# A fused attention and FNet layer on one core: fewer idle products ahead of the first latents, a z tile ahead of block one's columns, and pairs of halves that join the tile rotation one piece later

## The chip, the core and the metric

The kernel runs on one core of one Trainium2 chip. The metric is the device time of one execution in microseconds (us); less is better. PE is the matrix engine, DVE the vector engine, ACT the scalar engine, POOL GpSimd and SP the engine that issues most of the DMAs.

## The reference, cut to what matters

One layer, 512 latent tokens and 256 context tokens of 2048 channels, all in float32:

```
ada    = silu(c) @ w_ada + b_ada                    # 2048 -> 3*2048: shift, scale, gate
h      = rmsnorm(x, norm_g) * (1 + scale) + shift   # the latents, 512 x 2048
p      = h @ w_in                                   # q, k, v, z_a, u_b, z_b, g_a, g_b
q, k   = rope(rmsnorm(heads of p)); k, v also of the context
y_a    = (attention(q, k, v) * silu(z_a)) @ w_proj_a
y_b    = (fft2(u_b).real * silu(z_b)) @ w_proj_b
y      = (sigmoid(g_a) * y_a + sigmoid(g_b) * y_b) @ w_out
out    = rmsnorm(x + gate * y, final_g)
```

## The kernel before, in words

**Splitting.** PE gets float32 precision from three products of halves: every operand is split into a high half, which ACT rounds off (L176), and a low half, which DVE takes as the difference (L177). `mm3` (L327 to L329) is the three products. So each piece of weights (128 x 1024) goes through a DMA by SP or POOL, then ACT, then DVE, before PE can use it.

**The start stage**, to about 166 us. xT arrives and ACT and DVE square its rows, two at a time; DVE adds the two squares (L534), and PE adds up over the partitions with a column of ones (`token_norms`, four products of 128 columns for each of eight pairs, L536). Between them stand idle products whose results nobody reads (`warm`, L516, into the PSUM buffer `wacc`). Then come a square root on ACT (L540), a reciprocal on DVE (L541), the first half of the adaptive row for block 0 of the channels (`matvec(0, 0)`, L554), the spreading of the reciprocal root over the partitions (`spread`, L547), and `matvec(0, 1)`. With them `columns(0)` makes two columns, gain and shift (PE transposes in `turned` L575, DVE sums them up in `factors` L586 to L589), and `row_hi`, `scaled` and `row_lo` (L605, L608, L612) make the latents of block 0, high and low half. PE's products for u (four tiles) and z (four tiles, t = 4 to 7) of this block follow (`start_work`, L660 to L663 and L327 to L329). The z tiles go through the two PSUM buffers of `bank3`; `keep` (L635) moves each out, in block 0 by a copy on ACT (L641), later by an addition on DVE (L643). The same is done for blocks 1, 2, 3 and so on up to 15. `some(n)` issues the next n pieces of this work, `modulate(k, split_next)` the two matvecs of block k, a split of a loaded weight piece and the copy of the row (`ado`, L570). Here the order on PE, ACT and DVE is the order of the code, written out by hand (`tc.manual_schedule`).

**The eight groups** follow, g = 0 to 7: seven products with four pieces of weights each (28 pieces a group). PE works 2.74 us on a piece. The tile framework's scheduler sets the order here. A piece's halves are taken from a list that is rotated by one at each split (`hl_tiles`, L239): three pairs of whole tiles, to which at the step Q5 of group 0 two "int tiles" are added (`hl_pools += range(MORE_HL)` in the loop over the groups, MORE_HL = 2). An int tile is a pair of halves in two places, so a piece that gets one is split in two steps of 512 columns on each engine, and its rows are named `s` where those of the others are `whi` and `wlo`. From that point `get` splits up to four pieces ahead (`look`). At the step Q3 of group 4 the int tiles are taken out again, and at the start of group 6 they come back. Some pieces of weights are differences: DVE subtracts one loaded piece from another (L265) before the split, and gate rows are scaled on DVE (L1285) before their split.

Of the kernel before, what the change touches and what calls it, by code (L numbers as in the profile page):

```python
# [22 lines left out]
KK = D // P  # L23
# [96 lines left out]
def block_kernel(ctx, tc, xT, ctx_rows, ctx_toks, x, c_row, w_ss, w_gate, vecs, qkg, rope, dft_c, dft_s,  # L120
                 w_start, w_g, w_pab, w_o, final_g, out):
    nc = tc.nc
# [54 lines left out]
        return first, nc.vector.tensor_tensor(lo, src, hi.bitcast(F32), op=ALU.subtract)  # L177


    todo, ahead = [], []  # L180
    chain, left = [], [0] * 4
    raw_pools, hl_pools = [(wp, RAW, "raw", RAW)], [wp] * HL

# [53 lines left out]
        return [Halves([pairs[2 * n + k][i][:, :, 256:] for k in range(2)]) for i in range(2)]  # L237

    def hl_tiles():  # L239
        hl_pools.append(hl_pools.pop(0))  # L240
        pool = hl_pools[-1]
        if isinstance(pool, tuple):
            return [slot_tile(p, (1024,), F32R) for p in pool]
        if isinstance(pool, int):
            return int_tiles(pool)
        return [pool.tile([P, 1024], F32R, tag=t, bufs=hl_pools.count(pool), name=uid("w" + t)) for t in ("hi", "lo")]
# [266 lines left out]
    def warm(n, src):  # L513

        for _ in range(n):
            nc.tensor.matmul(wacc[:, :256], ones, src, start=True, stop=True)  # L516

    def token_norms():

        t = hm_tile([P, 2, T], F32, name=uid("nm"))  # L520
        pick, r = t[:, 0, :].rearrange("p (t c) -> p t c", t=4), t[:, 1, :P]
        nc.gpsimd.memset(pick, 0.0)
        for t in range(4):
            nc.gpsimd.memset(pick[32 * t : 32 * t + 1, t, :], 1.0)
        acc = bank2()
        for q in range(0, KK, 2):
            two = hm_tile([P, 2, T], F32, name=uid("sq"))
            a, b = two[:, 0, :], two[:, 1, :]
            nc.scalar.activation(a, xt[:, q, :], ACT.Square)
            if q in (6, 10):  # L530
                nc.vector.tensor_tensor(b, xt[:, q + 1, :], xt[:, q + 1, :], op=ALU.mult)
            else:
                nc.scalar.activation(b, xt[:, q + 1, :], ACT.Square)
            nc.vector.tensor_tensor(a, a, b, op=ALU.add)  # L534
            for t in range(4):
                nc.tensor.matmul(acc[32 * t : 32 * t + 32, :P], ones[:, :32], a[:, t * P : t * P + P],  # L536
                                 start=q == 0, stop=q == KK - 2)
            warm(2 if q < KK - 2 else 1, two[:, 0, :256])

        nc.scalar.activation(r, acc[:, :P], ACT.Sqrt, bias=eps_t[:, 0:1], scale=1.0 / D)  # L540
        nc.vector.reciprocal(r, r)  # L541
        return pick, r
# [60 lines left out]
    def row_hi(kb):  # L603
        rows_of(kb)
        nc.scalar.activation(hhi[kb], y_of[kb], ACT.Identity, bias=shift[:, kb, 0:1], scale=gain[:, kb, 0:1])  # L605

    def scaled(kb):
        nc.vector.tensor_scalar(xt[:, kb, :], y_of.pop(kb), gain[:, kb, 0:1], None, op0=ALU.mult)  # L608
# [26 lines left out]
    def keep(t, acc, kb, nk):  # L635
        if held and held[0] is None:
            held[0] = t, acc, kb, nk
            return
        dst = pt(t)
        if kb == 0 or t < 4:  # L640
            nc.scalar.copy(dst, acc)  # L641
        else:
            finals.append(nc.vector.tensor_tensor(dst, acc, dst, op=ALU.add))  # L643
# [41 lines left out]
    def some(n):  # L685
        for _ in range(n):
            next(work)
# [21 lines left out]

    E = mybir.EngineType  # L710
    with tc.manual_schedule(engines={E.PE}):
        norms = token_norms()
        two[0] = bank2()
        matvec(0, 0)
        rx0.append(spread(*norms))
        matvec(0, 1)
        with tc.manual_schedule(engines={E.Activation, E.DVE}):
            nc.scalar.copy(rx, rx0[0])
            by_root(0)
            split_next()  # L720
            taken(0)
            wada[2] = wada_load(2)
            load_start()
            columns(0)
            row_hi(0)
            scaled(0)
            row_lo(0)
            split_next()
            by_root(1)
            some(4)  # L730
            modulate(1, split_next)
            wada[3] = wada_load(3)
            load_start()
            some(2)
            columns(1)
            row_hi(1)
            scaled(1)
            row_lo(1)
            some(2)
            for kb in range(1, 4):  # L740
                k = kb + 1
                some(2 + (kb == 1))
                by_root(k)
                modulate(k, split_next)
                if kb < 3:
                    wada[k + 2] = wada_load(k + 2)
                    load_start()
                hold()
                some(2 - (kb == 1))
                columns(k)  # L750
                row_hi(k)
                release()
                scaled(k)
                if kb < 3:
                    some(2)
                row_lo(k)
                if kb == 3:
                    some(2)
                    by_root(5)
                    modulate(5)  # L760
                    for k in (6, 7):
                        wada[k] = wada_load(k)
                        load_start()
                    hold()
                    some(2)
                    columns(5)
                    row_hi(5)
                    release()
                    scaled(5)
                    row_lo(5)  # L770
                else:
                    some(2)
            for kb in range(4, KK - 4, 2):
                some(3)
                split_next()
                some(5)
                split_next()
                k = kb + 2
                for i in range(2):
                    modulate(k + i)  # L780
                    if k + 2 + i < KK:
                        wada[k + 2 + i] = wada_load(k + 2 + i)
                        for _ in range(2 if k + 2 + i == KK - 3 else 1):
                            load_start()
                some(1)
                for i in range(2):
                    turned(k + i)
                factors(k)
                make_h(k, lambda: some(1))
                factors(k + 1)  # L790
                make_h(k + 1, lambda: some(1))
                if k >= 8:
                    form_row(k - 8)
                    form_row(k - 7)
                some(1)
                if kb == KK - 6:
                    split_table(0)
                    split_from(get(("dftc", 0)), fch[:, 0, :], fch[:, 1, :])
                    load_start()
        some(2)  # L800
        k = KK - 2
        for i in range(2):
            modulate(k + i)
        some(1)
        for i in range(2):
            turned(k + i)
        for i in range(2):
            factors(k + i)
            ins = make_h(k + i)
            with behind(ins):  # L810
                split_next()
                form_row(k + i - 8)
            if not i:
                load_start()
        some(4)
        some(1)
        some(8)
# [499 lines left out]
    for g, kind in enumerate(KINDS):  # L1317
# [13 lines left out]
        for name in ONE_GROUP:  # L1331
# [5 lines left out]
            if (g, name) == (0, "P7"):  # L1337
                raw_pools.remove((rp, 1, "raw0", 1))
            if (g, name) == (0, "Q5"):
                hl_pools += range(MORE_HL)  # L1340
                look[0] = 4
            elif (g, name) == (0, "P2"):

                with tc.issue_after(last_split[-1][1].ins):
                    rotations(HD ** -0.5)
            elif (g, name) == (KV, "P1"):
                load_rotations(qkg[:, 2:4, :], nc.scalar)
            elif (g, name) == (KV, "Q5"):
                with tc.issue_after(last_split[-1][1].ins):
                    rotations(1.0)  # L1350
            elif (g, name) == (KV - 1, "Q3"):
                raw_pools.remove((rp, 1, "raw1", 1))
                hl_pools[:] = [p for p in hl_pools if not isinstance(p, int)]
            elif (g, name) == (KV + 1, "Q6"):
                raw_pools += [(rp, 1, "raw1", 1), (gvp, 2, "raw", 2)]
            elif (g, name) == (LAST, "P7"):
                raw_pools.remove((gvp, 2, "raw", 2))
            elif (g, name) == (LAST, "Q3"):

                free += [(fms[i], f"s{i}") for i in (4, 5, 6, 7, 12, 13, 14, 15, 8, 9, 10, 11, 2, 3, 0, 1)]  # L1360
                for h in range(2):
                    load_head(h)
            elif (g, name) == (LAST, "Q4"):
                hl_pools[:] = [p for p in hl_pools if not isinstance(p, int)]
                get_keys(0)
                jobs.append(lambda: turn_queries(0, pair("y")[:, 0, :]))
# [613 lines left out]
```

## Time and profile before

| | us |
|---|---|
| time before, three runs | 1307.32, 1310.15, 1310.84 (median 1310.15) |
| the profiled execution's own time | 1307.52 |
| its span | 1305.7 |
| PE busy in it | 1278.5 (98%) |
| DVE, ACT, POOL busy | 995.2, 683.6, 167.5 |
| mean granted clock of PE | 0.997 |
| first products with latents: block 0, block 1 | 25.95, 34.30 |

A row of a timeline reads: start, duration, engine, line, operation, output <- input with shapes, count, and in brackets how long the engine stood idle ahead of it and what ended that. A line of the waits reads: engine, what waited <- what for, us in total, times, longest. A line of the table of windows reads: from:to and length, then busy us (and count) of PE, its weight loads, DVE, ACT and POOL, the granted clock, the busy share of the DMA engines (a little over 1 where packets overlap) and GB/s. A line that a helper holds (L177 above all) stands for many places.

### The profile page before, as it was taken

To read this page: it belongs to the slowest core of one execution; us is meant where nothing else is said; L and a number is where in the kernel's file an instruction comes from. 1 tells how busy PE (TensorE), PEld (TensorE's weight loads), DVE (VectorE), ACT (ScalarE), POOL (GpSimd) and SP (SyncE) were. 2 spreads that over 40 slices of the span, in tenths; PEclk is the share of its full clock that TensorE was granted. 3 is DMA by queue.
4 is the path that set the end of the run, shared out by engine and by line. 5 is a ranking of instruction groups with operands and counts; after the bars stand their busy time and mean duration, and the time that the engine had idled before them with its cause. 6 is when DMAs were issued, how large, how long until landed. Compare 5 with 4: busy or idle time off the path is not lost.

```text
span 1305.7 us, 17712 instructions
## 1 busy us (share of the span) xinstructions
PE 1278.5 (98%) x6600; PEld 1051.8 (81%) x6600; DVE 995.2 (76%) x1301; ACT 683.6 (52%) x1078; POOL 167.5 (13%) x220
## 2 busy tenths in 40 slices
PE   7999999999999999999999999999999999999997
PEld 4676888888888788888888888888888888888885
DVE  4756899879687787658687756788798867887676
ACT  5322655555556455444355544666666646464544
POOL 0000011110202111011021010011110212221210
PEclk9999999999999999999999999999999999999998
DMA  9989487888889888977869897477862899998985
GB/s 377 367 353 358 164 244 190 228 238 281 203 276 263 232 299 271 313 200 186 270 202 275 282 227 264 155 229 244 241 230 81 236 248 249 244 212 229 222 204 171
DMA packets 104199, 318.56 MB, mean 244 GB/s; under 512 B 9872, under 2 KB 33040, under 8 KB 100144
## 3 DMA queue, kind: packets, MB, share of 16 engines
q1 hardware_dynamic: 55056, 197.86, 42.1%
q0 software_dynamic: 26736, 97.14, 34.9%
q10 hardware_dynamic: 22320, 22.42, 5.0%
q8 instruction: 52, 0.85, 0.2%
q14 instruction: 35, 0.29, 0.1%
HBM read 283.30 MB, written 34.09 MB: 243 GB/s over the span
## 4 chain that ended last, share of the span: by engine, by line
PE 84%; DMA 5%; DVE 5%; issue 4%; ACT 2%; POOL 0%; ACTq 0%; DVEq 0%; SPq 0%; POOLq 0%
PE banks L327 10%; PE banks L329 9%; PE banks L328 9%; PE x L328 7%; PE x L329 7%; PE x L327 7%; PE y L329 6%; PE y L327 6%; PE y L328 6%; PE pd L554 2%; PE banks L1468 2%; DMA wr<-in_w_g 2%; PE pb L327 1%; PE pb L329 1%; PE pb L328 1%
## 5 line engine op out<-in xcount | busy, mean ns | idle before, releaser
L176 ACT ACTIVATE whi<-R 128x1024 fp32r<-128x1024 f32 x138 | 145.2, 1058 | 134.8 <-PE banks L329 45.8
L177 DVE TENSOR_TENSOR wlo<-R,whi 128x1024 fp32r<-128x1024 f32 x138 | 167.5, 1221 | 55.4 <-ACT whi L176 55.1
L177 DVE TENSOR_TENSOR wlo<-wr,whi 128x1024 fp32r<-128x1024 f32 (+1 forms) x122 | 147.2, 1213 | 65.1 <-ACT whi L176 64.9
L176 ACT ACTIVATE whi<-wr 128x1024 fp32r<-128x1024 f32 (+1 forms) x122 | 127.4, 1051 | 120.4 <-PE y L329 35.5
L327 PE MATMUL banks<-whi,s 128*128 128x512 f32 x396 | 157.0, 396 | 3.2 <-DVE ev L1035 1.5
L328 PE MATMUL banks<-wlo,s 128*128 128x512 f32 x396 | 155.2, 392 | 0.0
L329 PE MATMUL banks<-whi,s 128*128 128x512 f32 x396 | 155.1, 392 | 0.0
L328 PE MATMUL x<-wlo,s 128*128 128x512 f32 x356 | 138.6, 389 | 1.5 <-DVE wlo L177 1.5
L327 PE MATMUL x<-whi,s 128*128 128x512 f32 x356 | 138.8, 390 | 0.0
L329 PE MATMUL x<-whi,s 128*128 128x512 f32 x356 | 138.6, 389 | 0.0
L327 PE MATMUL y<-whi,s 128*128 128x512 f32 x308 | 119.9, 389 | 0.6 <-DVE cxe L1188 0.6
L329 PE MATMUL y<-whi,s 128*128 128x512 f32 x308 | 119.8, 390 | 0.5 <-DVE s L177 0.5
L328 PE MATMUL y<-wlo,s 128*128 128x512 f32 x308 | 119.8, 389 | 0.0
L280 POOL DMA_DIRECT2D R<-in_w_g x64 | 55.9, 874 | 419.0 <-DVE wlo L177 260.3
L176 ACT ACTIVATE s<-wr 128x512 fp32r<-128x512 f32 (+2 forms) x95 | 61.0, 675 | 71.4 <-DMA wr<-in_w_g 22.3
L177 DVE TENSOR_TENSOR s<-wr,s 128x512 fp32r<-128x512 f32 (+2 forms) x95 | 68.0, 747 | 35.0 <-ACT s L176 34.2
L327 PEld LDWEIGHTS banks<-whi,s 128*128 128x128 f32 x396 | 74.4, 188 | 18.7 <-DVE R L1416 2.0
L329 PEld LDWEIGHTS banks<-whi,s 128*128 128x128 f32 x396 | 74.4, 188 | 15.5
L328 PEld LDWEIGHTS banks<-wlo,s 128*128 128x128 f32 x396 | 74.5, 188 | 14.1 <-DVE wlo L177 0.2
L328 PEld LDWEIGHTS x<-wlo,s 128*128 128x128 f32 x356 | 66.8, 188 | 15.7 <-DVE wlo L177 1.9
L327 PEld LDWEIGHTS x<-whi,s 128*128 128x128 f32 x356 | 66.9, 188 | 13.8
L329 PEld LDWEIGHTS x<-whi,s 128*128 128x128 f32 x356 | 66.8, 188 | 13.8
(312 smaller groups left out, 2824.0 us busy)
## 6 DMA issues: line engine op xcount, KB each, us to landing
wr<-in_w_g SPq DMA_DIRECT2D x128, 512.0 KB, 5.5
R<-in_w_g POOLq DMA_DIRECT2D x64, 512.0 KB, 7.3
wa<-in_w_ss SPq DMA_DIRECT2D x31, 1024.0 KB, 8.7
R<-in_w_g SPq DMA_DIRECT2D x32, 512.0 KB, 5.6
wr<-in_w_gate SPq DMA_DIRECT2D x32, 512.0 KB, 4.6
wr<-in_w_o SPq DMA_DIRECT2D x24, 512.0 KB, 7.5
R<-in_w_o POOLq DMA_DIRECT2D x24, 512.0 KB, 9.2
wr<-in_w_pab SPq DMA_DIRECT2D x20, 512.0 KB, 5.8
```

Source lines behind the costliest of these rows:

```text
L176: first = nc.scalar.activation(hi, src, ACT.Copy)
L177: return first, nc.vector.tensor_tensor(lo, src, hi.bitcast(F32), op=ALU.subtract)
L280: nc.gpsimd.dma_start(chain[e.pc], e.nxt, accum_op=ALU.add)
L327: nc.tensor.matmul(o, ah, bh, start=start, stop=False, skip_group_check=cont)
L328: nc.tensor.matmul(o, ah, bl, start=False, stop=False, skip_group_check=cont)
L329: nc.tensor.matmul(o, al, bh, start=False, stop=stop, skip_group_check=cont)
L554: nc.tensor.matmul(acc[32 * j : 32 * j + 32], c2[:, n, :], w[:, k, :], start=n < 4, stop=n >= KK - 4)
L1468: nc.tensor.transpose(tp[:, k * P : (k + 1) * P], p[:, k * P : (k + 1) * P], ident)
```

## The change

There are three edits. The first puts eight idle products of 128 columns at the head of PE's queue, and leaves one idle product of 256 columns behind each of the first six pairs of squares, where there were two behind each of the first seven and one behind the last. The second issues one z tile of block 0, not two, ahead of block 1's columns; the next one comes behind `row_hi(1)`, and its copy out of PSUM is made by DVE. The third lets the int tiles join the rotation one split later, which moves all later assignments of tiles to pieces by one, until the tiles go out in group 4.

```
     todo, ahead, more_hl = [], [], []
...
     def hl_tiles():
+        if more_hl and not more_hl[0]:
+            hl_pools.extend(range(MORE_HL))
+            more_hl.clear()
+        elif more_hl:
+            more_hl[0] -= 1
         hl_pools.append(hl_pools.pop(0))
...
     def warm(n, src):
         for _ in range(n):
-            nc.tensor.matmul(wacc[:, :256], ones, src, start=True, stop=True)
+            nc.tensor.matmul(wacc[:, : src.shape[-1]], ones, src, start=True, stop=True)
...
-            warm(2 if q < KK - 2 else 1, two[:, 0, :256])
+            if q < KK - 4:
+                warm(1, two[:, 0, :256])
...
         dst = pt(t)
-        if kb == 0 or t < 4:
+        if kb == 0 and t == 5:
+            nc.vector.tensor_copy(dst, acc)
+        elif kb == 0 or t < 4:
             nc.scalar.copy(dst, acc)
...
     with tc.manual_schedule(engines={E.PE}):
+        warm(8, ones)
         norms = token_norms()
...
-            some(2)
+            some(1)
             columns(1)
             row_hi(1)
+            some(1)
             scaled(1)
...
             if (g, name) == (0, "Q5"):
-                hl_pools += range(MORE_HL)
+                more_hl.append(1)
                 look[0] = 4
```

**First place, PE at the end of the sums.** `pd_157` is the sum over the squares (`pd_165` after the change), `s_208`, `s_218` and `s_228` are the last three pairs' squares, `pc_148` is the buffer of the idle products, and the L554 row is `matvec(0, 0)`. Before:

```order
L536 MATMUL pd_157<-s_208,ones 32x128 x4
L516 MATMUL pc_148<-s_208,ones 128x256 x2
L536 MATMUL pd_157<-s_218,ones 32x128 x4
L516 MATMUL pc_148<-s_218,ones 128x256 x2
L536 MATMUL pd_157<-s_228,ones 32x128 x4
L516 MATMUL pc_148<-s_228,ones 128x256
L554 MATMUL pd_239<-wa_121,c_136 32x256 x8
L547 MATMUL pc_248<-s_151 128x128 x4
```

The same place on PE after the change, where the squares are called `s_211`, `s_220` and `s_228`:

```order
L541 MATMUL pd_165<-s_211,ones 32x128 x4
L521 MATMUL pc_148<-s_211,ones 128x256
L541 MATMUL pd_165<-s_220,ones 32x128 x4
L541 MATMUL pd_165<-s_228,ones 32x128 x4
L560 MATMUL pd_238<-wa_121,c_136 32x256 x8
L553 MATMUL pc_247<-s_159 128x128 x4
```

Five idle products stood among these last sums, and one is left.

**Second place, PE around block 1's columns.** `wa_130` and `wa_132` are the two halves of block 1's row weights, `pc_341`, `pc_346` and `pc_360` the z tiles t = 4, 5 and 6 of block 0, and the L575 row turns block 1's row. Before:

```order
L554 MATMUL pd_312<-wa_130,c_136 32x256 x8
L554 MATMUL pd_312<-wa_132,c_136 32x256 x8
L327 MATMUL pc_341<-s_286,whi_291 128x512
L328 MATMUL pc_341<-s_287,whi_291 128x512
L329 MATMUL pc_341<-s_286,wlo_292 128x512
L327 MATMUL pc_346<-s_286,whi_291 128x512
L328 MATMUL pc_346<-s_287,whi_291 128x512
L329 MATMUL pc_346<-s_286,wlo_292 128x512
L575 MATMUL pd_312<-ident,ado_333 128x128 x2
L327 MATMUL pc_360<-s_286,whi_291 128x512
```

After the change on PE, where `pc_340` and `pc_352` are t = 4 and 5:

```order
L560 MATMUL pd_311<-wa_130,c_136 32x256 x8
L560 MATMUL pd_311<-wa_132,c_136 32x256 x8
L332 MATMUL pc_340<-s_285,whi_290 128x512
L333 MATMUL pc_340<-s_286,whi_290 128x512
L334 MATMUL pc_340<-s_285,wlo_291 128x512
L581 MATMUL pd_311<-ident,ado_332 128x128 x2
L332 MATMUL pc_352<-s_285,whi_290 128x512
L333 MATMUL pc_352<-s_286,whi_290 128x512
L334 MATMUL pc_352<-s_285,wlo_291 128x512
```

And DVE at that place after the change, from the split of the third weight piece to block 1's low half:

```order
L177 TENSOR_TENSOR wlo_329<-wr_134,whi_328 128x1024
L592 TENSOR_REDUCE adr_347<-pd_311 128x4
L593 TENSOR_SCALAR gain<-adr_347,bsc_98,small 128x2
L595 TENSOR_SCALAR shift<-adr_347,small 128x2
L647 COPY part<-pc_352 128x512
L614 TENSOR_SCALAR xt<-S_67,gain 128x512
L618 SCALAR_TENSOR_TENSOR s_286<-xt,shift,s_285 128x512
```

The turn moved ahead of tile t = 5, and the copy of that tile stands on DVE between the shift and the scaling; the other rows of DVE are those of before.

**Third place, DVE in group 3**, the pieces of the product P2 (their loads are `wr_3539`, `wr_3548`, `wr_3566` and `wr_3573`) and, behind them, the four differences of the next product but one, P7 (L265, from `R` and the loads `wr_3609` to `wr_3689`). `wlo_3612` is the first piece of the product Q6, which comes right behind P2. Before:

```order
L265 TENSOR_TENSOR wr_3609<-R_1324,wr_3609 128x1024
L177 TENSOR_TENSOR s_721<-wr_3566,s_720 128x2x256
L265 TENSOR_TENSOR wr_3689<-R_1327,wr_3689 128x1024
L265 TENSOR_TENSOR wr_3627<-R_1325,wr_3627 128x1024
L177 TENSOR_TENSOR wlo_3594<-wr_3573,whi_3593 128x1024
L265 TENSOR_TENSOR wr_3645<-R_1326,wr_3645 128x1024
L177 TENSOR_TENSOR wlo_3612<-R_1324,whi_3611 128x1024
```

After the change on DVE, where the loads have numbers lower by one (`wr_3572` is the last piece of P2, `wlo_3611` the first of Q6):

```order
L270 TENSOR_TENSOR wr_3608<-R_1323,wr_3608 128x1024
L177 TENSOR_TENSOR s_559<-wr_3572,s_558 128x2x256
L270 TENSOR_TENSOR wr_3688<-R_1326,wr_3688 128x1024
L177 TENSOR_TENSOR s_720<-wr_3572,s_719 128x2x256
L270 TENSOR_TENSOR wr_3626<-R_1324,wr_3626 128x1024
L270 TENSOR_TENSOR wr_3644<-R_1325,wr_3644 128x1024
L177 TENSOR_TENSOR wlo_3611<-R_1323,whi_3610 128x1024
```

The last piece of P2 gets an int tile, so that it is split in two steps, which stand behind the first and the second difference; all four differences stand ahead of the first split of Q6.

More of the change, by code (lines that the diff above doesn't have):

```diff
@@ L177, in split_from @@
         return first, nc.vector.tensor_tensor(lo, src, hi.bitcast(F32), op=ALU.subtract)
-    todo, ahead = [], []
+    todo, ahead, more_hl = [], [], []
     chain, left = [], [0] * 4
@@ L239, in hl_tiles @@
     def hl_tiles():
+        if more_hl and not more_hl[0]:
+            hl_pools.extend(range(MORE_HL))
+            more_hl.clear()
+        elif more_hl:
+            more_hl[0] -= 1
         hl_pools.append(hl_pools.pop(0))
@@ L515, in warm @@
         for _ in range(n):
-            nc.tensor.matmul(wacc[:, :256], ones, src, start=True, stop=True)
+            nc.tensor.matmul(wacc[:, : src.shape[-1]], ones, src, start=True, stop=True)
     def token_norms():
@@ L537, in token_norms @@
                                  start=q == 0, stop=q == KK - 2)
-            warm(2 if q < KK - 2 else 1, two[:, 0, :256])
+            if q < KK - 4:
+                warm(1, two[:, 0, :256])
         nc.scalar.activation(r, acc[:, :P], ACT.Sqrt, bias=eps_t[:, 0:1], scale=1.0 / D)
@@ L639, in keep @@
         dst = pt(t)
-        if kb == 0 or t < 4:
+        if kb == 0 and t == 5:
+            nc.vector.tensor_copy(dst, acc)
+        elif kb == 0 or t < 4:
             nc.scalar.copy(dst, acc)
@@ L711, in block_kernel @@
     with tc.manual_schedule(engines={E.PE}):
+        warm(8, ones)
         norms = token_norms()
@@ L733, in block_kernel @@
             load_start()
-            some(2)
+            some(1)
             columns(1)
             row_hi(1)
+            some(1)
             scaled(1)
@@ L1339, in block_kernel @@
             if (g, name) == (0, "Q5"):
-                hl_pools += range(MORE_HL)
+                more_hl.append(1)
                 look[0] = 4
```

## Prediction

> **What bounds the kernel now.** I begin with the busy shares on the page:
>
> ```profile
> PE 1278.5 (98%) x6600; PEld 1051.8 (81%) x6600; DVE 995.2 (76%) x1301; ACT 683.6 (52%) x1078; POOL 167.5 (13%) x220
> ```
>
> PE is busy for 98% of the span, so a change can gain only in three ways: by PE's idle time (27 us), by work of PE that nobody needs, or by a stage in which PE's work waits. The longest waits of PE say where the idle time lies:
>
> ```profile
> PE pd L536 <- DVE s L534: 7.0, 1, 7.0
> PE x L328 <- DVE wlo L177: 1.5, 1, 1.5
> ```
>
> 7.0 is the wait for the first pair of squares; 1.5 is one wait in group 3. The table of windows shows the start:
>
> ```profile
> 12.10:20.30 8.20, 8.20 (x75) 4.71 (x78) 3.00 (x6) 2.74 (x6) 0.00 (x0) 1.00 1.04 410
> 26.00:35.00 9.00, 8.78 (x61) 5.89 (x62) 5.16 (x9) 4.81 (x8) 0.00 (x0) 1.00 1.01 416
> 35.00:62.00 27.00, 27.00 (x216) 18.67 (x215) 19.26 (x39) 7.92 (x13) 0.00 (x0) 1.00 0.95 356
> ```
>
> From 12.1 to 20.3 PE is never idle, though its products are sums of squares and idle products: "busy" here is no limit by useful work. Through 35 the DMA engines are full (1.01 to 1.04), so loads land there when they do, however early PE is. Behind 35 PE is full with needed work: what the start gains is carried to the end, if later loads have room (0.95 and less).
>
> **The change, edit by edit.** *Idle products.* The timeline around the sums:
>
> ```profile
> 7.59 2.08 PE L516 MATMUL pc<-s,ones 128*128 128x256 f32 x4
> ...
> 15.18 0.69 DVE L534 TENSOR_TENSOR s<-s 128x512 f32<-128x512 f32 x1 [0.35 <-ACT s L533]
> 15.34 1.13 PE L516 MATMUL pc<-s,ones 128*128 128x256 f32 x4
> ...
> 19.24 0.42 PE L536 MATMUL pd<-s,ones 128*32 128x128 f32 x8
> 19.59 0.70 PE L516 MATMUL pc<-s,ones 128*128 128x256 f32 x2
> 19.73 0.37 ACT L540 ACTIVATE s<-pd,eps_t 128x128 f32<-128x128 f32 x1 [4.59 <-PE pd L536]
> 20.13 0.95 DVE L541 RECIPROCAL s<-s 128x128 f32<-128x128 f32 x1 [4.26 <-ACT s L540]
> 20.22 1.07 PE L554 MATMUL pd<-wa,c 128*32 128x256 f32 x16
> 21.23 1.15 PE L547 MATMUL pc<-s 128*128 128x128 f32 x8
> 22.31 1.07 PE L554 MATMUL pd<-wa,c 128*32 128x256 f32 x16
> ...
> 25.95 0.50 PE L660 MATMUL pb<-s,whi 128*128 128x512 f32 x1 [0.34 <-ACT s L605]
> ```
>
> (Each float32 product shows as two.) DVE has the last pair at 15.87 (15.18 + 0.69); PE sums it up only at 19.24, 3.4 late, because it works off idle products: two cost 1.13 behind sums of 0.42 (at the half clock of the first pairs 2.08). With one, a step at the full clock costs 0.42 + 0.57 = 1.0, less than the some 1.3 between the pairs that DVE delivers, so the queue is empty by the last pair whatever the first five leave. The eight new products stand in the 7.0 of waiting and cost nothing. Then the last sum ends at 15.87 + 0.48 = 16.35 (0.42, and 0.06 for the signal, as the root at 19.73 follows the sum's end at 19.66), the root at 16.8, the reciprocal at 17.75. `matvec(0, 0)` fits ahead of that. The spread runs from 17.87 to 19.0. `matvec(0, 1)` wants to start there. Its weights:
>
> ```profile
> 9.09 0.33 SPq L465 DMA_DIRECT2D wa<-in_w_ss  x1
> wa<-in_w_ss SPq DMA_DIRECT2D x1, 512.0 KB, 10.3
> ```
>
> They land at 19.39, which costs at most 0.35 more: 20.05 to 20.5 for its end in place of 23.38 (22.31 + 1.07). As the wait affects few of its products, I take 20.05, so everything behind it to the first latents moves by **3.33**: L660 at 22.62 in place of 25.95.
>
> *Block 1.* Not all of it arrives, since the next step hangs on loads:
>
> ```profile
> 13.62 0.33 SPq L465 DMA_DIRECT2D wa<-in_w_ss  x1
> wa<-in_w_ss SPq DMA_DIRECT2D x1, 1024.0 KB, 13.0
> ```
>
> ```profile
> 27.92 1.06 ACT L176 ACTIVATE whi<-wr 128x1024 fp32r<-128x1024 f32 x1 [1.29 <-DMA wr<-in_w_start]
> 28.92 1.93 PE L554 MATMUL pd<-wa,c 128*32 128x256 f32 x32
> 29.02 1.23 DVE L177 TENSOR_TENSOR wlo<-wr,whi 128x1024 fp32r<-128x1024 f32 x1 [0.79 <-ACT whi L176]
> 30.92 0.37 ACT L570 COPY ado<-pd 128x256 f32<-128x256 f32 x1 [1.94 <-PE pd L554]
> ...
> 32.28 0.38 PE L575 MATMUL pd<-ident,ado 128*128 128x128 f32 x2
> ...
> 32.77 0.18 DVE L586 TENSOR_REDUCE adr<-pd 128x4 f32<-128x16 f32 x1 [2.52 <-PE pd L575]
> ...
> 33.30 0.49 DVE L608 TENSOR_SCALAR xt<-S,gain 128x512 f32<-128x512 f32 x1
> 33.43 0.82 ACT L605 ACTIVATE s<-S,shift,gain 128x512 fp32r<-128x512 f32 x1 [0.36 <-DVE shift L589]
> ...
> 34.30 0.50 PE L660 MATMUL pb<-s,whi 128*128 128x512 f32 x1 [0.22 <-ACT s L605]
> ...
> 36.00 0.69 DVE L643 TENSOR_TENSOR part<-pc,part 128x512 f32<-128x512 f32 x1 [0.97 <-PE pc L663]
> ```
>
> `matvec(1)` would start at 28.92 - 3.33 = 25.6 and end at 27.65 (its second weights land at 26.62, in time). But the copy of its row stands on ACT behind the split of the third weight piece, and that waits for its load at 27.9 in before too, in a stretch where the DMAs are full. So ACT is free at 28.98, the row is there at 29.35 in place of 31.29, a gain of 1.94 and no longer 3.33. PE has finished t = 4 at 28.4 (27.65 and 0.7, since two such tiles lie between 30.85 and 32.28), waits 1.0, and turns the row by 29.7. In the old order it would turn at 29.35 anyway, behind t = 5. DVE is free of the low half at 30.25 (29.02 + 1.23), so the columns, some 0.6 of work (32.77 to 33.39), are ready at 30.8 in either order. That is what the edit runs into: the turn is earlier, the columns are not.
>
> Then the new order has t = 5 still to come: PE does it from 29.7 to 30.4, DVE copies it behind the shift. A copy from PSUM by DVE isn't in the trace. It lies between 0.49 (L608, one operand from SBUF) and 0.69 (L643, from PSUM, two operands); I take 0.69, the row that reads the same buffer, so 30.75 to 31.45. Tile t = 6 takes the other buffer meanwhile; t = 7 needs this one and ends at about 32.1. Only then comes L660 of block 1, whose latents stood ready at 31.65 (30.8 + 0.82). So L660 starts at 32.1, **2.2** ahead of 34.30: the edit itself loses up to 0.45 of what the earlier sums would give. With 0.49 it is 0.2 less. Behind the copy on DVE wait `scaled` and `row_lo`; the low half is wanted 0.95 after L660, so 0.7 there is covered.
>
> The Trainium skill ("VectorE: DVE Perf Modes", Mode 2×_2P) has one-operand copies in float32 go at twice the rate only from SBUF, as PSUM has one read port; at one element a cycle of 0.96 GHz, 512 elements are an estimated 0.53 us. By that t = 7 starts some 0.15 sooner, and the sum is 0.15 better.
>
> *The rotation.* The shift by one decides which pieces get two short splits in place of one long. It adds no split work to speak of (one row less on DVE here, one more there), so I look only where a split comes last. That is the 1.5 of the waits above:
>
> ```profile
> 423.33 1.23 DVE L265 TENSOR_TENSOR wr<-R,wr 128x1024 f32<-128x1024 f32 x1 [3.28 <-DMA wr<-in_w_g]
> 424.48 0.68 DVE L177 TENSOR_TENSOR s<-wr,s 128x512 fp32r<-128x512 f32 x1
> 425.08 2.35 DVE L265 TENSOR_TENSOR wr<-R,wr 128x1024 f32<-128x1024 f32 x2
> 427.35 1.22 DVE L177 TENSOR_TENSOR wlo<-wr,whi 128x1024 fp32r<-128x1024 f32 x1
> 428.62 0.50 PE L328 MATMUL x<-wlo,s 128*128 128x512 f32 x1 [1.50 <-DVE wlo L177]
> ```
>
> The last split of P2 (427.35) stands behind three subtractions that wait for loads. After the change its halves stand behind one and two: done at 425.1 and 426.9, before PE asks at 426.96. But now four subtractions and the two halves (4 x 1.14 + 2 x 0.60 from 423.33) stand ahead of Q6's first split: it starts at 429.1 and ends at 430.3, where PE, no longer held up, asks at 429.7. So 1.5 becomes 0.6: **-0.9**.
>
> The sum: -2.2 - 0.9 = -3.1, from 1307.52 to 1304.4. That execution lies 1.4 below the mean of the four times known (1308.96) and 2.6 below the median. I put the forecast on the mean: **1305.9**, 0.3% below the median of 1310.15.
>
> **The rivals.** *The loads do not hold block 1*: if the third piece lands sooner, the full 3.33 stays and the sum is -4.2: 1304.8. For it: in a full stretch one execution doesn't fix which load is served first. Against it: nothing that is issued ahead of this load changes. *The rotation gives nothing*, or one new wait of a like size: -2.2, so 1306.8. For it: every piece of groups 0 to 4 changes its place in DVE's queue, and I followed only waits and small reserves. *The change doesn't reach the latents*: the start is bound by landings alone, -0.5 at most: 1308.5.
>
> *Slower, by one late load.* In group 3 a raw buffer is turned round through DVE:
>
> ```profile
> 361.38 6.89 DMA wr<-in_w_g
> ```
>
> ```profile
> 371.00 1.22 DVE L177 TENSOR_TENSOR wlo<-wr,whi 128x1024 fp32r<-128x1024 f32 x1
> ```
>
> The load is issued when the gate piece (L1285) is done, lands 6.9 later, and is split at 371.00, and done at 372.2, some 3.05 before PE's first product with it at 375.3. The new order puts other DVE rows, which wait for PE's results, ahead of that gate piece. If that misses one turn, the price is 6.89 - 3.05 = 3.85, and -2.2 + 3.85 is +1.6, the 0.9 of this group lost with it: 1310.6. It decides from a delay of the issue of 5.3 (3.05 + 2.2). Two such turns give +5.5: 1314.5.
>
> *Slower, by the clock.* PE becomes thinner between 13.7 and 22.6, some 60% busy (5.5 of 8.9 by the rows above). In the trace a thinner stretch keeps the clock, and only an idle one loses it:
>
> ```profile
> 124.00:128.00 4.00, 2.01 (x36) 0.92 (x32) 2.37 (x4) 0.37 (x1) 0.00 (x0) 1.00 0.84 320
> ...
> 1298.90:1305.00 6.10, 0.00 (x0) 0.00 (x0) 1.58 (x3) 1.67 (x4) 0.00 (x0) 0.50 0.47 173
> ```
>
> Should the clock fall, the spread, the matvec and the turn double (1.15 + 1.07 + 0.38 = 2.6), and so do products for up to 5 us behind them, as long as the first ones took to raise it (from the end of PE's first wait, 7.0, to the window from 12.1 with its full price): 2.5 more. Then `matvec(1)` starts at 25.6 + 5.1 = 30.7, behind its loads, and L660 of block 1 at some 36.2, 1.9 later than before: +1.9 - 0.9 = +1.0, so 1310.0. The Trainium skill ("TensorE: Matmul & The Clock Gate", Part 1) has the clock start at half, reach the full rate after some 3.4 us of sustained work and fall after an idle window of as long. By it the eight idle products at the head may bring the full clock sooner, and no gap here is so long; the row of 124 to 128 agrees, and the sum stays.
>
> **How the numbers follow.** About 0.3% (3.9 us) is what a measurement here tells from no change; the bounds are 1306.2 and 1314.1. The forecast case has 0.42, no gain by the rotation 0.18, the full start 0.15, no effect 0.05, late loads 0.15 (one or two), the clock 0.05. The forecast lies beside the bound, so each case is spread over both sides by the 3.5 in which executions of one kernel lie (1307.32 to 1310.84): faster 0.43 (0.24 of the forecast, 0.12 of the full start, 0.07 of the third), slower 0.12 (0.07 of late loads, the rest from places that I haven't followed), same 0.45. The range reaches from 1302.6 (the full start at the level of the lowest execution, 1307.32 - 4.2 = 1303.1, and the edit of block 1 costing nothing, 0.45) to 1311.5 (one late load, 1310.6, and half the 1.9 by which the highest execution lies above the mean).
>
> **What would show it.** L536's last row at about 16.0, and the root right behind; L660 at 22.6 for block 0 and 32.1 for block 1; DVE's copy at 30.8, and PE waiting for it ahead of t = 7; ACT's split at 27.9 unmoved. In group 3 the wait of 1.5 gone and one of 0.6 in Q6. It is wrong if the PE waits hold a new row of over 1, if the granted clock shows 0.50 behind 13, or if the gain at 35 us isn't found again at 166.

## The result, and the profile after

The changed kernel took 1304.01 us (median of 6 runs, 1302.65 to 1305.56), the kernel before 1309.52 (6 runs, 1307.32 to 1311.1): a ratio of 0.9958, 95% interval 0.9945 to 0.9971, so 5.5 us less (3.8 to 7.2). The profiled execution took 1302.87, 4.65 less than that of before; its span is 1301.1. The forecast was 1305.9.

The start, in the timeline of the changed kernel, to be held against the rows shown of before:

```profile
15.29 0.69 DVE L539 TENSOR_TENSOR s<-s 128x512 f32<-128x512 f32 x1 [0.35 <-ACT s L538]
16.04 0.42 PE L541 MATMUL pd<-s,ones 128*32 128x128 f32 x8 [0.61 <-DVE s L539]
16.53 0.37 ACT L546 ACTIVATE s<-pd,eps_t 128x128 f32<-128x128 f32 x1 [1.27 <-PE pd L541]
16.91 1.07 PE L560 MATMUL pd<-wa,c 128*32 128x256 f32 x16 [0.45 <-DMA wa<-in_w_ss]
...
18.03 1.13 PE L553 MATMUL pc<-s 128*128 128x128 f32 x8
...
19.09 1.07 PE L560 MATMUL pd<-wa,c 128*32 128x256 f32 x16
...
22.73 0.50 PE L668 MATMUL pb<-s,whi 128*128 128x512 f32 x1 [0.34 <-ACT s L611]
```

The last sums follow DVE by 0.06, and PE now idles 0.61 ahead of them: the queue of idle products is gone. The first latents stand at 22.73 (25.95 before). Block 1 in the same view:

```profile
27.98 1.06 ACT L176 ACTIVATE whi<-wr 128x1024 fp32r<-128x1024 f32 x1 [4.57 <-DMA wr<-in_w_start]
...
28.94 0.35 ACT L576 COPY ado<-pd 128x256 f32<-128x256 f32 x1
29.07 1.23 DVE L177 TENSOR_TENSOR wlo<-wr,whi 128x1024 fp32r<-128x1024 f32 x1 [4.07 <-ACT whi L176]
...
29.35 0.44 PE L581 MATMUL pd<-ident,ado 128*128 128x128 f32 x2 [0.66 <-ACT ado L576]
...
30.61 0.22 DVE L595 TENSOR_SCALAR shift<-adr,small 128x2 f32<-128x2 f32 x1
30.74 0.68 DVE L647 COPY part<-pc 128x512 f32<-128x512 f32 x1
...
30.87 0.81 ACT L611 ACTIVATE s<-S,shift,gain 128x512 fp32r<-128x512 f32 x1 [1.08 <-DVE shift L595]
...
31.48 0.50 PE L332 MATMUL pc<-s,whi 128*128 128x512 f32 x1 [0.32 <-DVE part L647]
...
32.30 0.40 PE L668 MATMUL pb<-s,whi 128*128 128x512 f32 x1
```

ACT's wait for the load of the third piece grew from 1.29 to 4.57, and its split starts where it did. Block 1 begins at 32.30 in place of 34.30; of the 3.2 won at block 0, 2.0 are left. In group 3 DVE now looks like this:

```profile
420.05 1.23 DVE L270 TENSOR_TENSOR wr<-R,wr 128x1024 f32<-128x1024 f32 x1 [2.66 <-DMA wr<-in_w_g]
421.19 0.68 DVE L177 TENSOR_TENSOR s<-wr,s 128x512 fp32r<-128x512 f32 x1
421.80 1.22 DVE L270 TENSOR_TENSOR wr<-R,wr 128x1024 f32<-128x1024 f32 x1
422.93 0.68 DVE L177 TENSOR_TENSOR s<-wr,s 128x512 fp32r<-128x512 f32 x1
423.54 2.35 DVE L270 TENSOR_TENSOR wr<-R,wr 128x1024 f32<-128x1024 f32 x2
425.81 3.48 DVE L177 TENSOR_TENSOR wlo<-R,whi 128x1024 fp32r<-128x1024 f32 x3
```

This is the order that was read off (a half behind one subtraction, a half behind two, Q6's split behind all four), and no wait of PE of over 0.2 is left in groups 0 to 4, neither the 1.50 of P2 nor the 0.52 of group 0 nor one in Q6. One place in group 4 got worse. DVE there before, and then after the change:

```profile
533.68 1.23 DVE L177 TENSOR_TENSOR wlo<-wr,whi 128x1024 fp32r<-128x1024 f32 x1 [3.96 <-ACT whi L176]
534.82 1.22 DVE L1035 TENSOR_TENSOR ev<-ev,x 128x1024 f32<-128x1024 f32 x1
```

```profile
532.08 1.21 DVE L1045 TENSOR_TENSOR ev<-ev,x 128x1024 f32<-128x1024 f32 x1
533.21 1.22 DVE L177 TENSOR_TENSOR wlo<-wr,whi 128x1024 fp32r<-128x1024 f32 x1
```

An addition (L1035 before, L1045 after) now stands ahead of a split and not behind it, and PE's products behind that split come 0.5 later, though the idle time in the view is only 0.13.

How far the same product of PE is ahead of before, in the two traces: 2.0 at block 1, 1.8 at 154, 2.1 at 224, 3.9 at 432, 3.4 at 600, 3.8 at 622, 4.3 at 918, and 4.6 at the end. The start makes 2.0 to 2.1, groups 0 to 4 another 1.3 in all. The last 1.2 come at waits (near 621, 916 and behind 1100) that differ from one execution to the next: c_before below, the same program as before, gains 1.1 on it behind 600 as well.

### The profile page after: what moved, and what is told of

It reads as the page before. It is cut to its first block, busy times and chain, and to the rows that moved or that the text cites. A ratio compares the mean times of both kernels' runs of the same rounds, so it can differ in the third digit from the quotient of the medians.

```text
span 1301.1 us, 17699 instructions
## 1 busy us (share of the span) xinstructions
PE 1277.7 (98%) x6598; PEld 1051.0 (81%) x6598; DVE 994.4 (76%) x1301; ACT 683.8 (53%) x1076; POOL 167.6 (13%) x220
## 4 chain that ended last, share of the span: by engine, by line
PE 83%; DMA 6%; DVE 6%; issue 3%; ACT 1%; POOL 0%; SPq 0%; DVEq 0%; POOLq 0%; ACTq 0%
PE banks L332 10%; PE banks L333 10%; PE banks L334 10%; PE x L334 8%; PE x L333 8%; PE x L332 8%; PE y L334 6%; PE y L333 6%; PE y L332 6%; PE banks L1478 2%; PE pd L560 2%; DVE wlo L177 1%; PE pb L332 1%; PE pb L333 1%; PE pb L334 1%
## 5 line engine op out<-in xcount | busy, mean ns | idle before, releaser
L332 PE MATMUL x<-whi,s 128*128 128x512 f32 x352 | 137.1, 390 | 0.0
L334 PE MATMUL x<-whi,s 128*128 128x512 f32 x352 | 137.0, 389 | 0.0
L332 PE MATMUL y<-whi,s 128*128 128x512 f32 x316 | 123.0, 389 | 0.3 <-DVE cxe L1198 0.3
L333 PE MATMUL y<-wlo,s 128*128 128x512 f32 x316 | 123.1, 389 | 0.1
L334 PE MATMUL y<-whi,s 128*128 128x512 f32 x316 | 122.8, 389 | 0.0
```

Of the source, the lines that this page charges most:

```text
L332: nc.tensor.matmul(o, ah, bh, start=start, stop=False, skip_group_check=cont)
L333: nc.tensor.matmul(o, ah, bl, start=False, stop=False, skip_group_check=cont)
L334: nc.tensor.matmul(o, al, bh, start=False, stop=stop, skip_group_check=cont)
```

## The experiments

All times are ratios to the kernel before, run on the same chip beside it. "Block 1" is PE's first product with block 1's latents (34.30 in before). "P2" and "Q6" are PE's waits for a split in group 3, as idle time. Such a wait costs some 0.3 more than its idle time: around P2's 1.50 in before, PE's products start 1.89 and 0.34 apart, where 0.23 is the rule, so what is behind it comes 1.8 later.

| run | ratio, 95% interval | block 1 | P2 | Q6 |
|---|---|---|---|---|
| c_before | 0.9996, 0.9983 to 1.0009 | 33.64 | 1.44 | - |
| c_after | 0.9950, 0.9933 to 0.9967 | 32.05 | - | - |
| e1_sums | 0.9970, 0.9953 to 0.9986 | 31.66 | - | - |
| e1_again | 0.9969, 0.9956 to 0.9983 | 31.62 | 0.54 | - |
| e2_rot | 0.9989, 0.9973 to 1.0005 | 34.15 | - | 0.40 |
| e9_z_only | 0.9985, 0.9970 to 1.0000 | 34.07 | 1.75 | - |
| e3_no_z | 0.9967, 0.9951 to 0.9983 | 31.69 | - | 0.62 |
| e4_no_head | 0.9961, 0.9945 to 0.9977 | 33.00 | - | 1.05 |
| e8_no_idle | 0.9952, 0.9934 to 0.9970 | 32.39 | - | 0.21 |
| e5_act_copy | 0.9971, 0.9957 to 0.9986 | 32.94 | - | - |
| e6_cols_first | 0.9948, 0.9928 to 0.9968 | 31.37 | - | 0.22 |
| e6b_no_rot | 0.9951, 0.9934 to 0.9968 | 31.09 | 1.74 | - |

**e1_sums, e1_again: the idle products alone.** Of the diff only the lines on `warm`.

> Only the edit of the idle products (eight at the head, six between the sums). My theory: the last sum ends at about 16.4 and the first latents (L660 of before) stand at 22.7 in place of 25.95; block 1 is then held by the third weight piece's load at 27.9 and gets its first product at about 31.75 in the old order of the z tiles, 2.55 ahead of before's 34.30. The time falls by 2.2 to 2.6. Rival: the earlier turn is what carries the gain past the late load, so without it block 1 starts at 33 or later and the time falls by under 1.3.

> The edit of the idle products alone, a second time. If the wait of group 3 goes by the earlier start, it is under 0.5 again; if its absence was of that one execution, it is 1.0 to 1.5. Block 1 starts at 31.7 within 0.4 in both cases.

The timeline of e1_sums at block 1:

```profile
30.79 0.82 ACT L611 ACTIVATE s<-S,shift,gain 128x512 fp32r<-128x512 f32 x1 [0.59 <-DVE shift L595]
...
31.66 0.50 PE L666 MATMUL pb<-s,whi 128*128 128x512 f32 x1 [0.23 <-ACT s L611]
```

31.66 and 31.62 against 31.75 expected: the rival falls. The earlier sums alone give the whole gain at block 1 and 0.3% of the time. What was not expected is in group 3: P2's wait shrank to nothing and to 0.54 without the rotation. In the first of these profiles DVE runs some 2 further ahead of PE there, since the loads ahead of its subtractions, from 345 on, landed up to 1.2 sooner after their issue. The one that differs most, issued at 348.94 in before, took 6.47 and 6.62 in the two profiles of e1, and 7.65 to 8.09 in the four with the old rotation and a P2 wait of over 1.4.

**e2_rot: the rotation alone.**

```
+        if more_hl and not more_hl[0]:
...
-                hl_pools += range(MORE_HL)
+                more_hl.append(1)
```

> Only the rotation (int tiles one piece later). My theory as predicted: PE's wait of 1.5 in group 3 shrinks to 0.6, so -0.9. As the trace of the changed kernel reads: that wait is gone altogether, and half of the one in group 0 (0.52), so -2.1 behind group 3, with the start as in before (block 1 at 34.30). Rival: the waits go only because the start is earlier there, so the wait stays and the time changes by under 0.5.

PE's rows with a wait in groups 0 and 3, in e2_rot:

```profile
430.80 0.50 PE L333 MATMUL y<-wlo,s 128*128 128x512 f32 x1 [0.40 <-DVE wlo L177]
```

That is the wait in Q6 that the prediction had at 0.6; P2's is gone, with the start as in before. From 154 to 432 PE gained 1.5 on before, and lost 0.5 of it again in group 4. (Just ahead of 154 it had lost 1.0 to a load of `R` that ACT got at 143.07, at 142.19 in before; up to there the order of the rows is that of before.) So the waits go by the order of the splits, as predicted, and the rival falls; in time the interval reaches just over no change.

**c_before, c_after: both kernels again**, unaltered.

> The kernel before once more, for a second profile of the same program. If PE's wait of 1.50 in group 3 belongs to the program, as the prediction took it, it is there again at 1.3 or more, and so is the one of 1.27 near 915. If it is of that execution (loads that came late), it is under 1.0 or gone, and the gain that the prediction put down to the rotation was in part none of it. The start stands in both: block 1's first product at 34.3 within 0.4.

> The changed kernel once more, for a second profile. By the theory that the start is fixed by its order, block 1's first product stands at 32.3 within 0.4, with the wait for the copy on DVE (0.3) again, and the granted clock falls again at about 8.7 and rises at about 12.1. The waits in groups 0 to 5 may differ by 1 in either direction if they are of the execution.

PE's waits in c_before:

```profile
PE x L328 <- DVE wlo L177: 1.4, 1, 1.4
PE pd L554 <- DMA wa<-in_w_ss: 1.3, 1, 1.3
PE pd L554 <- DVE part L643: 1.0, 1, 1.0
...
PE y L329 <- DVE s L177: 0.5, 1, 0.5
```

P2's wait and the 0.51 of group 0 are there again in the same program. The wait near 915 is not of one size: 1.27 in before, 0.32 here, and between nothing and 1.84 in the other profiles. The start of before moved by 0.66 from one execution to the next, more than I allowed; that of the changed kernel by 0.25. The clock in c_before is taken up below.

**e3_no_z: the change without the z edit.**

```
-            some(1)
+            some(2)
             columns(1)
             row_hi(1)
-            some(1)
             scaled(1)
...
-        if kb == 0 and t == 5:
-            nc.vector.tensor_copy(dst, acc)
-        elif kb == 0 or t < 4:
+        if kb == 0 or t < 4:
```

> The change without its z edit (two z tiles ahead of block 1's columns, both copied by ACT). My theory: the columns are ready when they were (30.8), the two tiles behind them end sooner, and block 1 starts at about 31.75 in place of 32.30: 0.4 to 0.6 better than the full change. Rival: the earlier turn is worth something, and block 1 starts at 32.7 or later, 0.4 or more worse than the full change.

31.69, by 0.4 to 0.6 earlier than the full change (32.30 and 32.05): the z edit costs what was predicted, and the rival falls. The scatter of the start is as large as this, but counted from ACT's split of the third piece it drops out: 3.76 and 3.77 in e1_sums, e1_again and e3_no_z, which have the old order of the tiles, and 4.30 to 4.32 in four profiles with the new one, so 0.55. In time the two can't be told apart.

**e9_z_only: the z edit alone.**

> Only the z edit (one z tile ahead of block 1's columns, the next copied by DVE), with the idle products and the rotation of before. By the numbers of before: the turn comes at 31.6 in place of 32.28, the columns at 32.6 in place of 33.39 (DVE is free there, 30.25, unlike in the changed kernel), t = 5 is copied at 33.2, t = 7 ends at 34.0, and block 1's first product stands at 34.0 to 34.2 in place of 34.30: no more than 0.3 gained, within 0.2% in time. Rival: the earlier columns are worth their 0.8.

34.07 against 34.0 to 34.2: the rival falls. In this execution the first latents came 0.18 sooner than in before, though; counted from them, block 1 comes 8.30 later here and 8.35 or 8.36 later in before, c_before and e2_rot. So with the sums of before the edit wins 0.05 at block 1, and with the earlier sums it loses 0.55. The reason is DVE, which in before waits for the turn, and in the changed kernel is still at the low half of the third piece.

**e5_act_copy: t = 5 copied by ACT** (the second part of e3's diff alone).

> The changed kernel with t = 5 copied by ACT, behind block 1's high half, in place of DVE. My theory: the copy starts at 31.7 (behind the high half's 0.81 from 30.87) in place of 30.74, so t = 7 waits until 32.3 and block 1's first product stands at 33.0 in place of 32.2: 0.8 lost at that place. Rival: PE has enough else to do, under 0.3 lost.

The timeline of e5_act_copy:

```profile
32.14 0.50 PE L332 MATMUL pc<-s,whi 128*128 128x512 f32 x1 [1.03 <-ACT part L647]
...
32.94 0.40 PE L666 MATMUL pb<-s,whi 128*128 128x512 f32 x1
```

So with this order of the tiles the copy has to be DVE's: on ACT the wait ahead of t = 7 is 1.03 in place of 0.32.

**e4_no_head: without the eight idle products at the head; e8_no_idle: without any ahead of or between the sums** (the last two lines go in e8_no_idle only).

```
-        warm(8, ones)
         norms = token_norms()
...
-            if q < KK - 4:
-                warm(1, two[:, 0, :256])
```

> The change without the eight idle products at the head. In the trace of the changed kernel the granted clock rose at 5.25, fell at 8.66 and rose at 12.08. My theory: without the eight it is half until about 12.06, as in before, the sums still end within 0.2 of 16.46, since the queue is empty before the last pair, and the time is that of the full change within 0.3. Rival: the eight products bring the gain (the sums keep up because of the full clock from 5.25 to 8.66); without them the last sum ends at 17 or later and 0.6 or more is lost.

> The changed kernel with no idle product at the head or between the sums (the three behind the turn of block 0 stay). My theory: the sums alone (0.65 of every 1.4 at half clock) do not raise the clock, so the spread, the second matvec and the turn run at half rate: the first latents at 25 or later in place of 22.7, and block 1 at 34 or later in place of 32.3: 1.5 to 3 lost of the gain. Rival: the clock rises all the same by 16, since the sums keep PE half busy, and nothing is lost (within 0.4 at block 1).

In e4_no_head the last sums:

```profile
15.73 0.69 DVE L539 TENSOR_TENSOR s<-s 128x512 f32<-128x512 f32 x1 [0.35 <-ACT s L538]
...
16.47 0.43 PE L541 MATMUL pd<-s,ones 128*32 128x128 f32 x8 [0.61 <-DVE s L539]
...
28.70 1.06 ACT L176 ACTIVATE whi<-wr 128x1024 fp32r<-128x1024 f32 x1 [4.85 <-DMA wr<-in_w_start]
...
33.00 0.39 PE L668 MATMUL pb<-s,whi 128*128 128x512 f32 x1
```

They end at 16.90, 0.44 later than in the changed kernel, but still 0.05 behind DVE, which had its last pair 0.44 later in this execution. So the head brings nothing here. Block 1 at 33.00 lies 4.30 behind the split that waits for the load (28.70); in the changed kernel it is 4.32 (27.98), in c_after 4.31 (27.74), in e8_no_idle 4.31 (28.08). That is the plainest sign of what holds block 1.

In e8_no_idle the clock stayed at half until 19.59. PE's products:

```profile
16.66 1.93 PE L558 MATMUL pd<-wa,c 128*32 128x256 f32 x16 [0.23 <-DMA wa<-in_w_ss]
...
18.52 1.66 PE L551 MATMUL pc<-s 128*128 128x128 f32 x8
...
20.11 1.07 PE L558 MATMUL pd<-wa,c 128*32 128x256 f32 x16
...
23.74 0.50 PE L666 MATMUL pb<-s,whi 128*128 128x512 f32 x1 [0.34 <-ACT s L609]
```

The matvec and the spread pay 0.9 and 0.5, and the first latents come 1.0 later. But block 1 stands at 32.39, 0.1 to 0.3 later, since it waits for its load anyway, and the time is that of the changed kernel. My expectation of 1.5 to 3 lost fails; I had left out that cover. In e1_sums, too, the clock was at half until 14.88 and block 1 stands at 31.66 (31.62 in e1_again, where it rose at 11.13).

**e6_cols_first, e6b_no_rot: block 1's columns ahead of the split's low half,** with and without the rotation. In both, t = 5 is copied by ACT, as in e5_act_copy; `split_hi` is a new function, not shown, that issues ACT's half of a split and returns DVE's.

```
-            modulate(1, split_next)
+            modulate(1)
+            split_lo = split_hi()      # ACT's half of the split
...
             some(1)
             columns(1)
+            split_lo()                 # DVE's half
+            some(1)
             row_hi(1)
-            some(1)
```

> The changed kernel with block 1's row copied on ACT ahead of the split that waits for the load at 27.9, its columns on DVE ahead of that split's low half, and t = 5 copied by ACT ahead of block 1's high half. My theory (the row stands behind the late load on ACT, and the columns behind its low half on DVE): the turn comes at 28.5 in place of 29.35, the columns at 29.5 in place of 30.8, and block 1's first product at 31.2 in place of 32.30, behind t = 7: 1.1 better at that place. Rival: block 1 is held by its weights' load itself or by PE's z tiles, so it moves by under 0.4.

> The kernel with block 1's columns first (as in the run before it), but with the rotation of before. Block 1's first product stands at 31.4, as there. In groups 0 and 3, if the rotation is what removes the waits of 0.51 and 1.44 (of both profiles of before), both are there again, and 1.5 to 2.2 of the gain is gone behind group 3. If the earlier start removes the one in group 3, as the profile with the sums alone had it, only the 0.51 in group 0 is there, and the time is that with the rotation within 0.5.

The timeline of e6_cols_first:

```profile
28.01 0.37 ACT L576 COPY ado<-pd 128x256 f32<-128x256 f32 x1 [5.06 <-PE pd L560]
...
29.58 0.22 DVE L595 TENSOR_SCALAR shift<-adr,small 128x2 f32<-128x2 f32 x1
29.71 1.22 DVE L716 TENSOR_TENSOR wlo<-wr,whi 128x1024 fp32r<-128x1024 f32 x1
...
31.37 0.40 PE L666 MATMUL pb<-s,whi 128*128 128x512 f32 x1
```

Columns at 29.8 in place of 30.8, and block 1 at 31.37 (31.2 expected). The queues on ACT and DVE behind the late load were the limit, and taking the columns out of them gives 0.7 to 0.9. In time it is not told apart from the changed kernel (0.9948 and 0.9950), so no version here is shown to be better.

PE's waits in e6b_no_rot, the same kernel with the rotation of before:

```profile
PE x L333 <- DVE wlo L177: 1.7, 1, 1.7
...
PE y L334 <- DVE s L177: 0.5, 1, 0.5
```

Both waits are back, and the gain on before falls from 4.5 to 3.0 at 433. But e6_cols_first pays in group 4:

```profile
534.22 0.50 PE L333 MATMUL y<-wlo,s 128*128 128x512 f32 x1 [0.41 <-DVE wlo L177]
```

At 600 the gains are 3.7 and 3.0, so the rotation is worth 0.7 here, 1.0 counted from block 1. The wait of group 0 is 0.51 or 0.52 in all six profiles with the old rotation and in none of the eight with the new one. The addition ahead of the split near 534 is the other way round: it is in all eight with the new one, where it costs up to 0.75 (0.4 in the mean), and in none of the six. P2's wait is 1.44 to 1.75 in four profiles with the old one, but 0 and 0.54 in the two of e1. An earlier start isn't the reason, as e6b_no_rot starts earlier still. What brought the loads sooner in e1 stays open. In the measured times the rotation's part isn't seen: e6_cols_first and e6b_no_rot are alike, e1 and e3_no_z too.

## Why the prediction was right, and where its sizes were off

*The idle products*: right to 0.1. The last sums at 16.04 (16.0), the first latents at 22.73 (22.62). I had `matvec(0, 0)` free to start; it waited 0.45 for its load and ended at 17.98, with the spread at 18.03 for 17.87.

*Block 1*: right in its order of causes and to 0.2 in its end, 32.30 for 32.1. The load at 27.9 didn't move, the turn came by 29.8, the shift by 30.83, DVE's copy at 30.74 took 0.68, and PE waited 0.32 for it. That the copy from PSUM costs what the row of L643 costs (0.69) is borne out; the estimate of 0.53 by the rate in the Trainium skill ("VectorE: DVE Perf Modes", Mode 2×_2P) was too low by 0.15, as I counted the elements and no fixed cost; its point that PSUM doesn't give the double rate agrees. That the edit loses up to 0.45 against the old order of the tiles is shown by e3_no_z (0.55, counted from the split of the third piece).

*The rotation*: near in size, but partly by luck. Predicted -0.9, it is up to 600 -1.0 by e2_rot (from 154 on), -1.0 by e6_cols_first against e6b_no_rot and -1.3 by the two first traces (both from block 1 on). A single pair of executions doesn't fix it: between 154 and 600 the eight profiles with the new rotation gain 0.0 to 1.7 on before (1.1 in the mean), the six with the old one -1.0 to 1.9 (0.3 in the mean, raised by the two of e1). Four terms make it up. P2's wait was taken at its idle time, 1.5, and cost 1.8. The 0.52 of group 0 was left out of the working; it goes, and that brings 0.3. Q6's wait was put at 0.6, and by the starts of the products it costs 0 to 1.3, 0.5 in the mean. And the new wait in group 4, 0.4 in the mean, wasn't foreseen; it offsets what the first two add.

*The sum*: -3.1 was forecast, the profiled executions differ by 4.65. Up to 600 it is 3.4, where the start gave 2.0 to 2.1 of 2.2 and the rotation 1.3 of 0.9; the other 1.2 come behind 600, at waits that c_before gains on as well. By the medians 5.5 is gained, with 3.8 to 7.2 possible, so 3.1 lies below that interval. Start and rotation by the traces (1.3 to 2.25 and 1.0 to 1.3) make 2.3 to 3.6. Some 2 to 3 of the measured gain is not accounted for. The forecast time came nearer than its sum, since 1305.9 was counted from the mean of the known times and stands 4.2 below their median; and the stated range, 1302.6 to 1311.5, is wide beside a gain of 5.5.

*The rivals*: the full start fell (the load held). The change reaches the latents. No late load came in groups 2 and 3. A new wait did come, in group 4, but smaller than the one that it replaced. The clock's rival was priced wrongly: a clock at half until 19.59 (e8_no_idle) cost block 1 at most 0.3, not 1.9, because the wait for the load hides it.

## What to carry to other kernels

An engine that is 100% busy in a stretch may be busy with filler that stands in its queue ahead of the work on the path; compare when the input was ready with when the engine took it up. How much of such a gain arrives is read from the first load behind it that doesn't move with it. And where a copy waits behind a split that waits for a load, the order within that engine's queue is worth more than the choice of engine. A shift in a rotation moves everything until the rotation ends: here it took away a wait in group 3 and made one in group 4, so its gain has to be counted to the end.

## What the runs showed of the clock

The prediction held that a stretch with PE half busy keeps the clock. That is so for some phases only. The windows table of c_before around the wait for a load at 126, and of the changed kernel in the sums:

```profile
123.44:126.85 3.41, 1.48 (x24) 0.50 (x16) 2.82 (x6) 0.37 (x1) 0.00 (x0) 1.00 0.70 288
126.85:130.27 3.42, 3.00 (x19) 1.54 (x20) 0.00 (x0) 0.37 (x1) 0.00 (x0) 0.50 0.90 310
```

```profile
5.25:8.66 3.41, 1.15 (x14) 0.55 (x18) 1.38 (x2) 3.02 (x6) 0.00 (x0) 1.00 1.02 416
8.66:12.08 3.42, 3.42 (x24) 1.36 (x28) 2.39 (x4) 2.51 (x5) 0.00 (x0) 0.50 1.02 411
12.08:15.49 3.41, 3.35 (x38) 1.45 (x38) 2.47 (x5) 2.51 (x5) 0.00 (x0) 1.00 1.05 419
```

In all 14 profiles the granted clock changes only at multiples of 3.41 from one another, and its loss goes by PE's share of the window before. A window that was 43% busy (1.48 of 3.41) cost the next one half its clock, and set PE back by 1.4. The eight products at the head did raise the clock at 5.25, and the wait for the first pair of squares took it away again at 8.66 (34% busy). They raised it in five of the eight profiles that have them; in e5_act_copy, e6_cols_first and e6b_no_rot the window that held them was 67 to 75% busy (85% and more in the five), and the clock stayed at half until 10.3 to 12.8. At the full clock, no window of 43% or less kept it, and none of 49% or more lost it. In e5_act_copy one of 46% lost it (and another, at 1293.9, kept it), in e6b_no_rot 49% kept it:

```profile
911.60:915.00 3.40, 1.56 (x8) 0.99 (x7) 2.16 (x5) 3.38 (x7) 0.00 (x0) 1.00 0.89 164
915.00:918.40 3.40, 3.40 (x13) 2.91 (x12) 1.85 (x3) 0.99 (x2) 1.59 (x3) 0.50 0.64 187
```

```profile
422.40:425.80 3.40, 1.66 (x7) 1.04 (x8) 3.31 (x4) 1.01 (x2) 0.00 (x0) 1.00 0.49 157
425.80:429.20 3.40, 3.40 (x16) 2.79 (x17) 3.40 (x4) 0.73 (x1) 0.71 (x1) 1.00 0.50 154
```

The Trainium skill ("TensorE: Matmul & The Clock Gate", Part 1) has free-running windows of this length, which agrees, and the clock go back after an idle one; here one less than half busy was enough. Where the windows fall differs from execution to execution (5.25 and 8.66 in the changed kernel, 3.95 and 7.36 in its second profile), so the two waits near 124 cost 1.4 more in c_before and nothing in before, which is the same program. Of the other profiles only e8_no_idle lost the clock there. That is a part of the scatter of the times: among the 79 runs of the kernel before that stand beside the experiments, the 22 with a mean granted clock of 0.996 or less took 1311.1 in the mean, the 57 with more 1308.8. Within each of the two sets the times still lie 8 or more apart, so it is not the whole.
